# A two-layer decoder step on one core: layer norms moved behind the next projection, the input taken in quarters, a bias table written later

## The chip, the cores and the metric

The kernel runs on one core of a Trainium2 chip. A core has a matrix engine (TensorE, PE in the rows, with its weight loads as PEld), VectorE (DVE), ScalarE (ACT), GpSimd (POOL), and SyncE (SP), which here only issues transfers. All of them work on SBUF; PE writes its sums to PSUM. Sixteen DMA engines move data to and from HBM for the queues of SP, ACT and POOL. The metric is the device time of one execution in microseconds, smaller is better.

## What is computed

A decoder trunk of two layers is applied to 256 prompt rows and 64 sample rows (8 sequences of 8), 320 columns in the transposed layout that the kernel keeps (`NT = 320`); the width of the model is 2048, that is 16 tiles of 128 features. Cut to what matters:

```
layer 0: q,k,v,qi,ki,wi = h @ a_w_in; an indexer scores the keys, keeps the top k; attention; @ a_w_o
h = LN(alpha*h + mixer(h))
h = LN(alpha*h + down(silu(dwconv3(h @ w_gate)) * (h @ w_up)))        # d_ff 5504
shared k,v = h @ b_w_kv
layer 1: q = h @ b_w_q (three head groups); dilated window attention on the shared k,v; @ b_w_o
h = LN(alpha*h + mixer(h));  h = LN(alpha*h + ConvFFN(h))
LN(x) = (x - mean(x)) * rsqrt(var(x) + eps) * g + b                   # over the 2048 features
```

Everything is fp32. A T5 bias by distance (a table `rel_bias` of 32 buckets for each of 16 heads) is added to the attention logits.

## The kernel before

All projections run through one class, `Stream` (L40). A job is one projection's column block of 256 (or 512) weight columns; it is cut into chunks of 4 of the 16 feature tiles (`kc=4`), 512 KB each. `load` fetches a chunk into `raw` on the SP queue, `split` turns it into a rounded part on ACT (L82) and a remainder on DVE (L84, the tile `hl`), and `run` issues three matmuls for each 128 x 128 block: high weight by high input, high by low, low by high (L123 to L125), each over 320 columns, in fp32r, added up in a PSUM tile `acc`. A full chunk is 24 such matmuls. Up to three split and three raw chunks stand ahead of the one in work. When the last chunk of a column block is done, the job's `epi` takes `acc` out of PSUM.

Everything else is written as generators, called lanes. `run` calls `steps()` twice in each chunk, and each lane then goes on by its rate, so that attention, table building and norms stand between the chunks of the stream. A scheduler then orders each engine's instructions and may put one ahead of another; what is marked `keep_in_program_order` stays where it was written. In each engine the instructions are then executed in that order.

The order of the jobs: the indexer's keys `ki` (80 columns), its queries `qi` (4 jobs), k and v (4), q (8); then layer 0's attention over gathered pages, which uses no stream; `wo` (8 jobs); the feed-forward, in which 11 groups of up jobs (gate and up halves) alternate with 8 down jobs each; then the shared k and v (`kvb`, `vb`), 24 `qb` jobs with layer 1's attention in lanes; `wo`; the second feed-forward; and the output.

The start (L1325 to L1358): x is loaded in twelve transfers, then all 16 feature tiles are transposed by PE (48 transposes, L1353), copied by ACT to `x32` (L1354), rounded by DVE to `xh`, and the remainder goes to `xl`. Then the first job, `ki`, runs. `gen_tables` makes the bias table `tr` (16 heads by 2312 distances) and writes it to DRAM in three forms: `trd`, eight shifted copies `bsa`, and `tb` (L1380), in which each head's 384 values stand 128 times, 3 MB. Layer 0's heads read `tb` much later.

The norms: the residual `R` gets each finished column block added on DVE (L502 in `wo`, L586 in the feed-forward), and running sums `s1` (values, DVE) and `s2` (squares from ACT, added on POOL). `ln_end` (L355) reduces the sums over partitions with small matmuls (L367, L371); `ln_finish` (L376) makes mean and 1/deviation, spreads them over the partitions with more of them (L388), and `normalise` then does, tile by tile, the subtraction on DVE or POOL (L409), the scaling (L410, DVE), `xh` (L412, ACT), the shifted value (L413, ACT) and `xl` (L414, DVE). The next job multiplies `xh` and `xl`. Three norms stand before a projection in this way: after layer 0's `wo`, after its feed-forward, and after layer 1's `wo`. The fourth is followed only by the output. `ln_prepare` (L327) multiplies `R` by alpha for the next residual.

## Time and profile before

| | |
|---|---|
| time, median of 3 runs | 3316.67 us (3316.25 to 3317.85) |
| profiled execution: time, span | 3318.17 us, 3316.0 us |
| mean granted clock of TensorE | 0.981 of 2.4 GHz |
| busy: PE, PEld | 3226.7 us (97%), 3058.1 us (92%) |
| busy: DVE, ACT, POOL | 1832.6 us (55%), 1364.1 us (41%), 623.8 us (19%) |
| HBM read, written | 542.14 MB, 17.59 MB |

PE is busy for nearly all of the span, but a busy PE is not always a PE at its full rate: matmuls are pipelined (one of 320 columns lasts 0.31 us in a row and the next one starts 0.147 us later), and the granted clock is one of two levels, 1.0 (2.4 GHz) or 0.5 (1.2 GHz). So what counts is how many matmuls a stretch holds, not how busy it is.

### The profile page before, as it was taken

What the parts mean: (1) busy time and instruction counts of PE and PEld (TensorE: products, weight loads), DVE (VectorE), ACT (ScalarE), POOL (GpSimd) and SP (SyncE); (2) the same over time, 40 slices, a digit from 0 to 9 for tenths busy, and PEclk for the clock granted to TensorE, in tenths of its full rate; (3) what the DMA queues carried; (4) which work ended last, traced back from release to release, by engine and by line L of the source; (5) the groups of instructions that cost most, each with busy time, mean ns of one, the idle gap of its engine ahead of it and who ended that gap; (6) DMA issues with size and microseconds to landing.
All of it is one profiled execution on the core that took longest, in us unless ns stands there. A gap on an engine that the chain in (4) does not pass through costs nothing.

```text
span 3316.0 us, 58328 instructions
## 1 busy us (share of the span) xinstructions
PE 3226.7 (97%) x23574; PEld 3058.1 (92%) x23574; DVE 1832.6 (55%) x3170; ACT 1364.1 (41%) x2209; POOL 623.8 (19%) x820
## 2 busy tenths in 40 slices
...
GB/s 186 146 174 163 254 309 296 164 105 166 148 152 147 152 150 149 152 148 152 139 238 160 221 190 199 206 199 171 105 160 148 152 148 152 149 151 150 149 152 139
DMA packets 543249, 562.75 MB, mean 170 GB/s; under 512 B 24598, under 2 KB 520926, under 8 KB 538806
## 3 DMA queue, kind: packets, MB, share of 16 engines
...
q8 instruction: 186, 3.05, 0.4%
q14 instruction: 83, 0.68, 0.1%
HBM read 542.14 MB, written 17.59 MB: 169 GB/s over the span
## 4 chain that ended last, share of the span: by engine, by line
PE 89%; DVE 4%; DMA 3%; ACT 1%; issue 1%; POOL 0%; SPq 0%; DVEq 0%; ACTq 0%; POOLq 0%
PE acc L123 26%; PE acc L124 26%; PE acc L125 26%; PE kt L1260 1%; DMA vtb<-in_cache_v_b_dram 1%; PE s L1057 1%; PE acc L1078 1%; PE s L1213 1%; PE oa L1129 1%; DMA kx<-in_cache_kidx_a_dram,i 1%; PE s L1160 1%; DVE hl L84 1%; PE ob L1303 1%; DVE R L410 1%; DVE w L852 0%
## 5 line engine op out<-in xcount | busy, mean ns | idle before, releaser
L84 DVE TENSOR_TENSOR hl<-raw,hl 128x1024 fp32r<-128x1024 f32 (+1 forms) x752 | 927.6, 1234 | 870.8 <-ACT hl L82 867.8
L82 ACT ACTIVATE hl<-raw 128x1024 fp32r<-128x1024 f32 (+3 forms) x770 | 804.3, 1045 | 1316.9 <-PE acc L125 1123.4
L123 PE MATMUL acc<-xh,hl 128*128 128x320 f32 (+1 forms) x4176 | 1316.5, 316 | 6.6 <-ACT xh L412 5.1
L124 PE MATMUL acc<-xl,hl 128*128 128x320 f32 (+1 forms) x4176 | 1299.9, 311 | 7.2 <-DVE xl L414 7.2
L125 PE MATMUL acc<-xh,hl 128*128 128x320 f32 (+1 forms) x4176 | 1297.9, 311 | 1.5 <-POOL hl L84 1.1
L123 PEld LDWEIGHTS acc<-xh,hl 128*128 128x128 f32 (+1 forms) x4176 | 790.1, 189 | 31.0 <-issue 20.8
L124 PEld LDWEIGHTS acc<-xl,hl 128*128 128x128 f32 (+1 forms) x4176 | 789.7, 189 | 15.2 <-DVE xl L414 12.5
L125 PEld LDWEIGHTS acc<-xh,hl 128*128 128x128 f32 (+1 forms) x4176 | 789.3, 189 | 6.0 <-issue 3.5
L124 PE MATMUL acc<-H,hl 128*128 128x320 f32 x1376 | 425.4, 309 | 1.1 <-POOL H L568 1.1
L123 PE MATMUL acc<-H,hl 128*128 128x320 f32 x1376 | 426.1, 310 | 0.0
L125 PE MATMUL acc<-H,hl 128*128 128x320 f32 x1376 | 425.3, 309 | 0.3 <-DVE hl L84 0.3
L124 PEld LDWEIGHTS acc<-H,hl 128*128 128x128 f32 x1376 | 258.3, 188 | 1.6 <-POOL H L568 1.6
L125 PEld LDWEIGHTS acc<-H,hl 128*128 128x128 f32 x1376 | 258.3, 188 | 0.6 <-DVE hl L84 0.6
L123 PEld LDWEIGHTS acc<-H,hl 128*128 128x128 f32 x1376 | 258.2, 188 | 0.1
L586 DVE TENSOR_TENSOR R<-R,acc 128x320 f32<-128x320 f32 x352 | 169.9, 484 | 122.0 <-PE acc L125 121.8
L551 POOL COPY gl<-E 128x2 f32<-128x2 f32 x86 | 24.8, 288 | 1039.4 <-ACT E L547 1039.4
L568 POOL TENSOR_TENSOR H<-h,H 128x320 fp32r<-128x320 f32 x86 | 106.1, 1235 | 452.5 <-ACT H L567 438.3
L123 PE MATMUL acc<-oh,hl 128*128 128x320 f32 x512 | 161.6, 317 | 0.5 <-ACT oh L994 0.5
L124 PE MATMUL acc<-ol,hl 128*128 128x320 f32 x512 | 160.0, 313 | 0.9 <-DVE ol L995 0.9
L125 PE MATMUL acc<-oh,hl 128*128 128x320 f32 x512 | 160.0, 313 | 0.0
L1150 POOL TENSOR_TENSOR bm<-tt,pmb 128x256 f32<-128x256 f32 x48 | 45.4, 971 | 327.1 <-DVE mxb L943 310.8
L123 PEld LDWEIGHTS acc<-oh,hl 128*128 128x128 f32 x512 | 96.7, 189 | 2.8 <-ACT oh L994 1.2
(391 smaller groups left out, 3176.8 us busy)
## 6 DMA issues: line engine op xcount, KB each, us to landing
...
```

Of the source, the lines that this page charges most:

```text
L82: a = self.nc.scalar.activation(out=hl[:, 0, :m], in_=raw[:, :m], func=AF.Copy)
L84: b = eng.tensor_sub(hl[:, 1, :m], raw[:, :m], hl[:, 0, :m].bitcast(F))
L123: nc.tensor.matmul(acc[:cw, :NT], hi, xh, start=st, stop=False)
L124: nc.tensor.matmul(acc[:cw, :NT], hi, xl, start=False, stop=False)
L125: nc.tensor.matmul(acc[:cw, :NT], lo, xh, start=False, stop=sp)
L410: ve.scalar_tensor_tensor(r, r, lnp[:, d, which:which + 1], pr if d < 2 else rstd, OP.mult, OP.mult)
L568: ge.tensor_sub(lo, h, hi.bitcast(F))
L586: ve.tensor_add(r, r, acc[:, :NT])
L1057: te.matmul(p[32 * g:32 * g + 32, :], S["qsf"][:, b, 32 * g:32 * g + 32], kts[g], start=False, stop=True, tile_position=(0, 32 * g))
L1078: te.transpose(p[:, 128 * i:128 * i + 128], kr[:, o:o + 128], idf)
L1129: te.matmul(o[32 * g:32 * g + 32, 0:128], ptq[:, 128 * t + 32 * g:128 * t + 32 * g + 32], v, start=(q == 0 and t == 0), stop=(q == 4), til ...
L1150: ge.tensor_add(bm[:, g, :], tt, S["pmb"][:, g, :])
```

## The change

1. **Norms behind the projection.** The up, `kvb`, `vb` and `qb` jobs no longer take the normalised input. They take `rh` and `rl`, the two parts of the residual times the norm's gain `g`, that need no mean and no deviation (`scale_hi` on ACT, `scale_lo` on DVE), and two more columns, `g` and `b` themselves, so their matmuls have `NX = 322` columns. When a column block is done, `fix` multiplies it by 1/deviation (DVE) and adds minus mean over deviation times the product of the weights with `g` (DVE, a second instruction); the product with `b` goes in as a bias of the next step. `ln_stats` makes the statistics in a lane while the next projection runs; `ln_rest` makes the normalised residual, times alpha, later, in a lane of its own. `ln_finish` and the feed-forward's `ln_prepare` are gone. The last norm, before the output, stays as it was.
2. **x in quarters.** x is loaded in four quarters of 512 features on three queues (SP, ACT, POOL), and the first projection is now `s0`, a job of 256 indexer query columns and the 80 key columns together. After the first two quarters are transposed, its chunks alternate with the transposes of the other two. The quarters are also written to DRAM for the residual straight from ACT's queue, and the scaling of `rb` by DVE, which `tr` needs, is done there.
3. **The bias table.** `tb` is no longer written from SBUF in `gen_tables`, but by one transfer from `trd` (DRAM to DRAM), at the sixth of the eight q jobs.

Smaller ones go with these: layer 1's mixer no longer runs `ln_prepare`, the squares are added on DVE (not POOL) during `wo`, `gen_tables_b` starts after the first up jobs, and layer 1's first loads of the k and v windows are pinned.

The core of the diff:

```diff
+NX = NT + 2
...
-                    nc.tensor.matmul(acc[:cw, :NT], hi, xh, start=st, stop=False)
-                    nc.tensor.matmul(acc[:cw, :NT], hi, xl, start=False, stop=False)
-                    nc.tensor.matmul(acc[:cw, :NT], lo, xh, start=False, stop=sp)
+                    nx = job.nx
+                    nc.tensor.matmul(acc[:cw, :nx], hi, xh, start=st, stop=False)
+                    nc.tensor.matmul(acc[:cw, :nx], hi, xl, start=False, stop=False)
+                    nc.tensor.matmul(acc[:cw, :nx], lo, xh, start=False, stop=sp)
...
+    S["mr"] = sel.rearrange("p j h q -> p (j h q)").bitcast(F)[:, 0:2 * NT].rearrange("p (k n) -> p k n", k=2)
...
+    def mv_r(k):
+        lo_upto(k + 1)
+        return S["rh"][:, k, :], S["rl"][:, k, :]
+
...
-    for j in range(4):
+    job("s0", W_in, [(A_QI, 256), (A_KI, 80)], KD, mv_x, lambda i, t: epi_ki(t) if i else epi_qi(0, t))
...
             if wide:
-                job(("up", l, f0, "w"), Wu, cols[:2], KD, mv_x, lambda i, t, f0=f0: epi_up(l, f0, i, t))
+                job(("up", l, f0, "w"), Wu, cols[:2], KD, mv_r, lambda i, t, f0=f0: epi_up(l, f0, i, t), nx=NX)
             for a in range(2 if wide else 0, len(cols), 2):
                 for i in range(2):
-                    job(("up", l, f0, a + i), Wu, [cols[a + i]], KD, mv_x,
-                        lambda _, t, f=f0 + a, i=i: epi_up(l, f, i, t))
+                    job(("up", l, f0, a + i), Wu, [cols[a + i]], KD, mv_r,
+                        lambda _, t, f=f0 + a, i=i: epi_up(l, f, i, t), nx=NX)
...
+    def scale_hi(d):
+
+        se.activation(out=S["rh"][:, d, 0:NT], in_=S["R"][:, d, :], func=AF.Identity,
+                      scale=lnp[:, d, S["which"]:S["which"] + 1])
+
+    def scale_lo(d):
+        ve.scalar_tensor_tensor(S["rl"][:, d, 0:NT], S["R"][:, d, :], lnp[:, d, S["which"]:S["which"] + 1],
+                                S["rh"][:, d, 0:NT].bitcast(F), OP.mult, OP.subtract)
...
+    def lo_upto(n):
+        while S["nlo"] < n:
+            d = S["nlo"]
+            if d % 4 == 0:
+                scale_gb(d, 4)
+            scale_lo(d)
+            S["nlo"] += 1
...
+    def ln_stats(rate, mode=None):
+
+        yield
+        yield
+        tk = S["rb"]
+        ve.memset(tk, 0.0)
+        pm, pv = ps("pm"), ps("pv")
+        for p, x in ((pm, S["s1"]), (pv, S["s2"])):
+            for t, n in TG:
+                te.matmul(p[:n, t:t + 1], x[:, 128 * t:128 * t + n], ones_d[:, 0:1], start=True, stop=True)
+        m, v, rs = tk[:, 0:3], tk[:, 4:7], tk[:, 8:11]
+        for t, n in ((slice(0, 2), 128), (slice(2, 3), 64)):
+            ve.tensor_scalar(m[:n, t], pm[:n, t], -1.0, None, OP.mult)
+            ve.tensor_copy(rs[:n, t], pv[:n, t])
+        ve.tensor_mul(v, m, m)
+        ve.tensor_sub(rs, rs, v)
+        se.activation(out=rs, in_=rs, func=AF.Sqrt, bias=epst)
+        ve.reciprocal(rs, rs)
+        ve.tensor_mul(m, m, rs)
+        yield
+        yield
+        for k, x in enumerate((m, rs)):
+            p = ps("mr")
+            for t, n in TG:
+                te.matmul(p[:, 128 * t:128 * t + n], x[:n, t:t + 1].to_broadcast([n, 128]), idf[:n, :n],
+                          start=True, stop=True)
+            se.activation(out=S["mr"][:, k, :], in_=p[:, :NT], func=AF.Copy)
+        S["norm"] = lanes.add(ln_rest(mode), rate)
+        yield
+
+    def ln_rest(mode):
+
+        R, w = S["R"], S["which"]
+        for d in range(KD):
+            r = R[:, d, :]
+            ag, ab = lnq[:, d, w:w + 1], lnq[:, d, 2 + w:3 + w]
+            ve.scalar_tensor_tensor(r, r, ag, S["mr"][:, 1, :], OP.mult, OP.mult)
+            ve.scalar_tensor_tensor(r, S["mr"][:, 0, :], ag, r, OP.mult, OP.add)
+            se.activation(out=r, in_=r, func=AF.Identity, bias=ab)
+            if mode == "xs" and d % 4 == 3:
+                a = d - 3
+                se.dma_start(out=xs[1][:, a * NT:(a + 4) * NT], in_=R[:, a:a + 4, :].rearrange("p k n -> p (k n)"))
+            yield
+
+    def fix(acc, t):
+
+        if S["stats"] in lanes.lanes:
+            lanes.drain(S["stats"])
+        uv = const.tile([128, 2], F, name="uv", tag="uv", bufs=4)
+        se.activation(out=uv, in_=acc[:, NT:NX], func=AF.Copy)
+        ve.tensor_mul(t, acc[:, :NT], S["mr"][:, 1, :])
+        ve.scalar_tensor_tensor(t, S["mr"][:, 0, :], uv[:, 0:1], t, OP.mult, OP.add)
+        return uv[:, 1:2]
...
-        sq = S["fp"].tile([128, NT], F, name="sq", tag="sq", bufs=3)
+        if pool:
+            sq = S["fp"].tile([128, NT], F, name="sq", tag="sq", bufs=3)
+        else:
+            sq = ps("sq")[:, :NT]
...
-        ge.tensor_add(S["s2"], S["s2"], sq)
+        (ge if pool else ve).tensor_add(S["s2"], S["s2"], sq)
...
-        def normalise(d):
-            r = R[:, d, :]
-            if d < 2:
-                ve.tensor_sub(r, r, pm)
-            else:
-                ge.tensor_sub(r, r, m1)
-            ve.scalar_tensor_tensor(r, r, lnp[:, d, which:which + 1], pr if d < 2 else rstd, OP.mult, OP.mult)
-            bias = lnp[:, d, 2 + which:3 + which]
-            se.activation(out=S["xh"][:, d, :], in_=r, func=AF.Identity, bias=bias)
-            se.activation(out=r, in_=r, func=AF.Identity, bias=bias)
-            ve.tensor_sub(S["xl"][:, d, :], r, S["xh"][:, d, :].bitcast(F))
-            if mode == "xs" and d % 4 == 3:
-                a = d - 3
-                sy.dma_start(out=xs[1][:, a * NT:(a + 4) * NT], in_=R[:, a:a + 4, :].rearrange("p k n -> p (k n)"))
...
     def epi_wo(l, p, accs):
         for i, acc in enumerate(accs):
             d = 2 * p + i
             r = S["R"][:, d, :]
             ve.tensor_add(r, r, acc[:, :NT])
-        ln_pair(p)
+        while S["nhi"] < min(2 * p + 2, 6 * p - 18):
+            scale_hi(S["nhi"])
+            S["nhi"] += 1
+        ln_pair(p, False)
 
...
@@ -541,11 +611,14 @@
         for i, acc in enumerate(accs):
             f = f0 + i
             stc = S["stc"][:, f, :]
+            x = Fp.tile([128, NT], F, name="fx", tag="fx", bufs=4)
+            v = fix(acc, x)
+            xp, xs_ = x[:, 0:256], x[:, 256:320].rearrange("p (b t) -> p b t", t=8)
             if kind == 0:
                 e = S["E"][f % 4]
                 es = e[:, 258:338].rearrange("p (b t) -> p b t", t=10)
-                se.activation(out=e[:, 2:258], in_=acc[:, 0:256], func=AF.Copy)
-                se.activation(out=es[:, :, 2:10], in_=acc[:, 256:320].rearrange("p (b t) -> p b t", t=8), func=AF.Copy)
+                se.activation(out=e[:, 2:258], in_=xp, func=AF.Identity, bias=v)
+                se.activation(out=es[:, :, 2:10], in_=xs_, func=AF.Identity, bias=v)
                 ge.tensor_copy(es[:, :, 0:2], stc[:, 0:16].rearrange("p (b t) -> p b t", t=2))
                 gl = S["gl"][:, f // 7, :, f % 7]
                 ge.tensor_copy(gl[:, 0:2], e[:, 256:258])
...
                 h = Fp.tile([128, NT], F, name="h", tag="h", bufs=3)
-                ve.tensor_mul(h[:, 0:256], c[:, 0:256], acc[:, 0:256])
-                ve.tensor_mul(h[:, 256:320].rearrange("p (b t) -> p b t", t=8), c_sample(c),
-                              acc[:, 256:320].rearrange("p (b t) -> p b t", t=8))
+                ve.scalar_tensor_tensor(h[:, 0:256], xp, v, c[:, 0:256], OP.add, OP.mult)
+                ve.scalar_tensor_tensor(h[:, 256:320].rearrange("p (b t) -> p b t", t=8), xs_, v, c_sample(c),
+                                        OP.add, OP.mult)
...
-            ln_pair(p)
+            ln_pair(p, True, out=l)
 
...
+        S["stats"] = lanes.add(ln_stats(0.7), 1.0)
+        lanes.add(gen_lo(), 1.0)
         for key in [k for k in jobs if isinstance(k, tuple) and k[0] in ("up", "down") and k[1] == l]:
-            if key[0] == "up" and key[2] == FGROUPS[0] and prep is None:
-                prep = lanes.add(ln_prepare(), 1.0)
+            if key[0] == "down" and key[2] == key[3] == 0:
+                if S["norm"] in lanes.lanes:
+                    lanes.drain(S["norm"])
+                ln_begin_sums()
+                if l == 0:
...
-        next(g)
-        return g
+        S["stats"] = lanes.add(ln_stats(0.8, "xs"), 1.0)
+        lo_upto(4)
+        lanes.add(gen_lo(), 1.3)
+        return True
...
+    def x_load(a, b):
+        for i in (sy.dma_start(out=xn[0][:, a:b], in_=x_prompt[0, 0:128, a:b]),
+                  se.dma_start(out=xn[1][:, a:b], in_=x_prompt[0, 128:256, a:b]),
+                  ge.dma_start(out=xn[2][:64, a:b], in_=xsf[:, a:b])):
+            tc.keep_in_program_order(i)
+
+    x_load(0, 512)
+    st.load(0)
+    x_load(512, 1024)
+    st.load(1)
...
+    def x_chunk(c):
+
+        for i in range(4):
+            k = 4 * c + i
+            p = ps("xt")
+            for t in range(3):
+                n = min(128, NT - 128 * t)
+                te.transpose(p[:, 128 * t:128 * t + n], xn[t][:n, 128 * k:128 * k + 128], idf[:n, :n])
+            x = x32[c][:, i, :]
+            se.activation(out=x, in_=p[:, :NT], func=AF.Copy)
+            ve.tensor_copy(S["xh"][:, k, :], x)
+            ve.tensor_sub(S["xl"][:, k, :], x, S["xh"][:, k, :].bitcast(F))
+        se.dma_start(out=xs[0][:, 4 * c * NT:4 * (c + 1) * NT], in_=x32[c].rearrange("p k n -> p (k n)"))
+
+    warm(10)
+    x_chunk(0)
+    x_load(1024, 1536)
+    warm(4)
+    x_chunk(1)
+    tc.keep_in_program_order(ve.tensor_scalar(rb, rb, 1.0 / SCALE, None, OP.mult))
+    x_load(1536, 2048)
+    run("s0", 2)
+    x_chunk(2)
+    run("s0", 4)
+    x_chunk(3)
+    run("s0", 6)
...
-        sy.dma_start(out=tb, in_=tr[:, 1800:2184].unsqueeze(1).to_broadcast([16, 128, 384]))
-        yield
...
+        if j == 5:
+            tc.keep_in_program_order(sy.dma_start(out=tb, in_=trd[:, 1800:2184].unsqueeze(1).to_broadcast([16, 128, 384])))
```

On PE, from the last down job of layer 0 to `kvb`, the kernel before has this order (`acc` is a projection's sum, `H` the feed-forward's activations, `pm`, `pv`, `m` and `rstd` the norm's small tiles):

```order
L125 MATMUL acc<-H,hl 128x320
L367 MATMUL pm<-zero 128x4
L367 MATMUL pv<-zero 128x4
L371 MATMUL pm<-ones_d,s_8116 64x1
...
L371 MATMUL pv<-ones_d,sq 128x1 x2
L388 MATMUL m_16425<-idf,tk 128x64
...
L388 MATMUL rstd<-idf,tk 128x128 x2
L123 MATMUL acc<-xh,hl 128x320 x4
L124 MATMUL acc<-xl,hl 128x320
```

and the changed one this:

```order
L127 MATMUL acc<-H,hl 128x320
L125 MATMUL acc<-rh,hl 128x322
L126 MATMUL acc<-rl,hl 128x322
...
L388 MATMUL pm<-ones_d,s_8395 64x1
L388 MATMUL pm<-ones_d,s_8395 128x1 x2
L388 MATMUL pv<-ones_d,s_8396 64x1
...
L403 MATMUL mr<-idf,rb 128x64
L403 MATMUL mr<-idf,rb 128x128 x2
```

The norm's small matmuls, which stood between the two projections, now stand inside the second one: 36 of its matmuls come before the first group of six, and 28 more before the second; at the other two norms it is much the same.

On DVE, in that last group of down jobs, the kernel before has for one job (`s1` is the running sum, `gln` belongs to an output of the convolution):

```order
L84 TENSOR_TENSOR hl_16098<-raw_15990,hl_16098 128x1024
L216 COPY gln_16094<-gt_16117 126x128
L586 TENSOR_TENSOR R_6390<-R_6390,acc_16103 128x320
L352 TENSOR_TENSOR s1_8116<-s1_8116,R_6390 128x320
L586 TENSOR_TENSOR R_6390<-R_6390,acc_16104 128x320
L352 TENSOR_TENSOR s1_8116<-s1_8116,R_6390 128x320
```

and the changed one:

```order
L85 TENSOR_TENSOR hl_16631<-raw_16492,hl_16631 128x1024
L663 TENSOR_TENSOR R_6405<-R_6405,acc_16636 128x320
L356 SCALAR_TENSOR_TENSOR rl_16521<-R_6405,lnp_83,rh_16520 128x320
L663 TENSOR_TENSOR R_6405<-R_6405,acc_16637 128x320
L449 TENSOR_TENSOR s1_8395<-s1_8395,R_6405 128x320
L218 COPY gln_16532<-gt_16677 126x128
L449 TENSOR_TENSOR s1_8395<-s1_8395,R_6405 128x320
L356 SCALAR_TENSOR_TENSOR rl_16521<-R_6405,lnp_83,rh_16520 128x320
```

The making of `rl` has moved up into the down jobs: eight of the 16 tiles stand before the last residual is added, where no such instruction stood before.

At the start, PE has in the kernel before all 48 transposes `xt` and then `ki` (80 columns). In the changed one it has 30 of them, the last six of which belong to the third quarter, ahead of the first product:

```order
L1460 MATMUL xt<-idf,xn_110 128x64
L1460 MATMUL xt<-idf,xn_108 128x128 x3
L1460 MATMUL xt<-idf,xn_109 128x128 x3
L125 MATMUL acc<-xh,hl 128x320
L126 MATMUL acc<-xl,hl 128x320
```

So the first product moves from the 49th place behind the warming matmuls to the 31st.

## Rows read from the trace of the kernel before

**Rows 1.** Stretches (us), matmuls writing `acc` alone: length, PE busy (count), PEclk, DMA, GB/s.

```profile
0.00:60.00 60.00, 26.60 (x146) 0.77 0.70 212
692.25:740.00 47.75, 31.55 (x180) 0.75 0.25 69
1624.00:1680.00 56.00, 42.58 (x252) 0.82 0.69 205
2362.65:2420.00 57.35, 46.53 (x280) 0.85 0.31 91
```

**Rows 2.** Stretches by engine: PE, PEld, DVE, ACT, POOL busy (count), PEclk, DMA, GB/s.

```profile
715.00:1595.00 880.00, 880.00 (x5989) 879.87 (x5988) 464.10 (x625) 355.51 (x492) 80.09 (x169) 1.00 0.51 150
...
1624.00:1645.00 21.00, 16.21 (x68) 13.84 (x68) 15.00 (x22) 10.97 (x21) 13.94 (x15) 0.56 0.16 59
...
1597.00:1625.00 28.00, 27.72 (x192) 27.65 (x192) 24.37 (x41) 14.61 (x26) 16.04 (x14) 1.00 0.56 164
...
1645.00:2200.00 555.00, 548.13 (x4382) 506.81 (x4382) 274.45 (x624) 225.31 (x391) 74.84 (x106) 1.00 0.69 200
...
110.00:138.00 28.00, 26.33 (x186) 21.83 (x184) 24.32 (x70) 16.93 (x36) 8.99 (x6) 1.00 0.88 111
...
138.00:149.00 11.00, 5.40 (x25) 3.52 (x24) 5.58 (x24) 4.04 (x10) 3.40 (x4) 0.69 1.00 272
```

**Rows 3.** Timeline of PE, norm before `kvb`: start, us, instruction, count, [idle before <-releaser].

```profile
1627.59 1.31 PE L371 MATMUL pv<-ones_d,sq 128*64 128x1 f32 x6
...
1630.59 1.84 PE L388 MATMUL rstd<-idf,tk 64*128 64x64 f32 x6
...
1634.13 1.44 PE L123 MATMUL acc<-xh,hl 128*128 128x320 f32 x4 [1.70 <-ACT xh L412]
...
1638.15 0.64 PE L124 MATMUL acc<-xl,hl 128*128 128x320 f32 x1 [2.58 <-DVE xl L414]
```

**Rows 4.** Timeline of PE at the start of the kernel.

```profile
14.28 10.45 PE L1353 MATMUL xt<-idf,xn 64*128 64x64 f32 x34 [0.30 <-DMA xn<-in_x_sample_dram]
...
27.83 0.55 PE L125 MATMUL acc<-xh,hl 128*80 128x320 f32 x1 [1.13 <-POOL hl L84]
...
47.56 1.03 PE L1370 MATMUL tr<-oneh,rb 32*16 32x512 f32 x2 [3.18 <-DVE rb L1363]
...
50.16 0.47 PE L123 MATMUL acc<-xh,hl 128*128 128x320 f32 x1
...
50.42 0.47 PE L124 MATMUL acc<-xl,hl 128*128 128x320 f32 x1
```

**Rows 5.** Timelines of SP's queue, ACT and PE around the writing of `tb`.

```profile
109.79 0.68 SPq L1380 DMA_DIRECT2D tb<-tr  x1
```

```profile
142.19 0.42 ACT L764 ACTIVATE khl<-kx 128x256 fp32r<-128x256 f32 x1 [9.17 <-DMA kx<-in_cache_kidx_a_dram,i]
```

```profile
143.86 0.47 PE L771 MATMUL kt<-idr,khl 128*128 128x128 f32 x2 [5.60 <-ACT rl L782]
```

**Rows 6.** Timeline of PE, two neighbouring fp32r matmuls of 512 columns.

```profile
124.12 0.49 PE L779 MATMUL sx<-kis,qh 128*128 128x512 f32 x1
124.45 0.39 PE L780 MATMUL sx<-kis,ql 128*128 128x512 f32 x1
```

**Rows 7.** Groups of DVE instructions by line and shape: count | busy us, mean ns | idle before.

```profile
L84 DVE TENSOR_TENSOR hl<-raw,hl 128x1024 fp32r<-128x1024 f32 x720 | 899.9, 1251 | 852.9 <-ACT hl L82 849.9 <-ACT rl L782 1.1 <-DMA vtb<-in_cache_v_b_dram 0.4
...
L586 DVE TENSOR_TENSOR R<-R,acc 128x320 f32<-128x320 f32 x352 | 169.9, 484 | 122.0 <-PE acc L125 121.8
...
L410 DVE SCALAR_TENSOR_TENSOR R<-R,lnp,rstd 128x320 f32<-128x320 f32 x48 | 36.9, 806 | 2.4 <-ACT rstd L392 2.4
...
L339 DVE SCALAR_TENSOR_TENSOR R<-R,sh 128x320 f32<-128x320 f32 x64 | 29.3, 504 | 0.0
```

**Rows 8.** Timeline of PE, second matmul on the last group's third tile, layer 0.

```profile
1597.28 0.42 PE L124 MATMUL acc<-H,hl 128*128 128x320 f32 x1 [1.06 <-POOL H L568]
```

214 lines of the change are left out of this document (110 added, 104 removed).

## The prediction

> **What bounds the kernel now.** The table of busy time was read first: PE is busy for 97% of the span, no other engine for more than 55%. That alone does not say that PE runs at its rate, so the second view was a list of long stretches, and there the number of matmuls was read, not the busy time. In the first feed-forward 5989 matmuls take 880 us, 0.1469 us each, at the full clock, 2.4 GHz [rows 2]. By its jobs the kernel issues 18,192 matmuls of 320 columns in its projections; at 0.1469 us they make 2672 of the 3316 us. The reader is to see that a stretch costs too much exactly where its length is more than its count times 0.1469 us.
>
> The third view puts that to the three norms that stand before a projection [rows 1]. After layer 0's `wo`: 47.75 us with 180 projection matmuls, 47.75 - 26.4 = 21.3 us lost. Before `kvb`: 56 us with 252, 19.0 lost. After layer 1's `wo`: 57.35 us with 280, 16.2 lost. Together 56.5 us. The timeline shows what they are made of: small matmuls of the statistics, which wait for DVE and ACT in turn; waits of PE of 1.70 us for `xh` and 2.58 us for `xl`; and a clock that fell, so that the next products run slowly [rows 3], granted 0.56 over 21 us [rows 2]. A matmul of 320 columns starts 0.26 to 0.27 us after the one before at the lower level, 1.2 GHz, as at 50.16 and 50.42 [rows 4].
>
> The start is the fourth place: the products come steadily only from 27.83 us, and up to 60 us only 146 were made, worth 21.4 us [rows 1, 4]. The fifth is the `tb` write, and the wait behind it [rows 5].
>
> **The change part by part.** The sum is made against the profiled execution, 3318.17 us, which is 1.5 us above the median of the runs.
>
> *The three norms.* The next projection no longer waits for mean and deviation, and if nothing took their place the 56.5 us would go. What comes back: twelve small matmuls a norm, in place of twenty. Six took 1.31 us and six 1.84 us in rows at about half the clock [rows 3]; at the full one I take half, 1.6 us, three times: 4.7. PE would wait next for `rl`, which DVE must make before the second matmul of a block. Layer 0's last down group has DVE busy for 24.37 of 28 us [rows 2], and eight of the sixteen `rl` tiles now come before its end: 8 x 0.504 to 8 x 0.806 us, 4.0 to 6.4 us [rows 7], where 3.6 are free. So DVE ends 0.4 to 2.8 us late, and with the splits of `kvb` crowding in as much as 6; I take 2.5, and 1 at each other norm, where the sums of squares moved from POOL to DVE. Net 56.5 - 4.7 - 4.5 = 47 us saved; bounds 35 and 53. If the cover is gone (PE with nothing to multiply until the statistics end) the old loss returns.
>
> *The two columns.* 322 columns in place of 320 for the up jobs (86 tiles x 48 x 2 layers = 8256), `kvb` and `vb` (384) and `qb` (2304): 10,944 matmuls. At 0.1469/320 us a column, two columns are 0.92 ns, 10 us in all. The trace has no matmul of 322 columns. Below it could be nothing. For the upper end: two neighbouring ones of 512 columns start 0.33 us apart [rows 6], (0.33 - 0.147)/192 = 0.95 ns a column, 1.9 ns for two, 21 us. I take 10, since nearly all of these run in rows like the first of [rows 2].
>
> The page "SBUF — State Buffer" of the Trainium skill, section "Door 1: The DMA port swizzle", speaks against this part: SBUF is read in lines of 16 bytes, and each step to a new line costs something. A block of 322 values of four bytes does not start on such a line every time. No row here shows what that costs; the fourth rival weighs it.
>
> *The fix.* Each tile of up, `kvb`, `vb` and `qb` now needs two more DVE instructions: one that reads PSUM, like L586 (0.484 us), and one like L339 (0.504 us), 0.99 us [rows 7]. In a feed-forward 86 tiles: 85 us on top of 464 in 880 us [rows 2], 62% full. PE hides it, 0 us, at most 10 if the accumulators come free late. In the `qb` stretch 48 x 0.99 = 47 us come on top of 274 in 555 us [rows 2], cost 1 us, 0 to 5. Not hidden is the end of each feed-forward: PE waits 1.06 us for `H` of the last group [rows 8], and the fix stands in just that chain. Two tiles, 2 x 0.99 us, twice: 4 us, 0 to 8.
>
> *x in quarters.* Before, the 34 last transposes run from 14.28 us at 10.45/34 = 0.31 us each [rows 4], so 14 were done by then. With 30 ahead of the first product, and the first two quarters landing no later, the same pace gives 14.28 + 16 x 0.31 = 19.2 us; with three queues and no wait for the second quarter about 17.5. From 27.83 that is 8.6 to 10.3 earlier. The 18 other transposes now stand between the products and still cost PE 18 x 0.15 to 18 x 0.31, 2.8 to 5.5 us. The wait for `rb`, 3.18 us [rows 4], goes with the scaling moved ahead, and with it the slow matmuls after it, from 49.6 to 53 us, some 14 x 0.12 = 1.7 us. Against it stand the splits and roundings that DVE must now do between the chunks, 2 us by choice. 9.5 - 4.2 + 3.2 + 1.7 - 2 = 8 us saved, bounds 4 (products at 19.2, DVE twice as late) and 16 (DVE never late, transposes at the full clock, and the 20 products that ran at the lower clock from 27.83 on, 2.4 us, faster too). The transfer of the third quarter stands on ACT's queue behind ACT's copies; if it lands late, PE waits and the clock falls.
>
> *The table.* `tb` is asked for at 109.79 us; the DMA engines are 88% busy up to 138 us, and ACT waits 9.17 us for the gathered `kx`, PE 5.60 us in turn [rows 5, 2]. Then the clock is granted at 0.69 over 11 us [rows 2]; I put 2 us on it. 7.5 saved, 3 to 9. In its new place the write stands on SP's queue among the loads of the q jobs. It takes some 32 us (109.79 to 142), in which the stream wants 512 KB per 24 matmuls, that is per 3.5 us. Up to six chunks are ahead, 21 us; if nothing else got through, 32 - 21 = 11 us would be lost. The burst moved 111 GB/s [rows 2], where another stretch reaches 272, so both share: I take 1, bounds 0 and 11. What is queued behind it on SP is the next `raw` loads, and PE waits for those.
>
> **Sum.** 3318.2 - 47 + 10 + 4 + 1 - 8 - 7.5 + 1 = 3271.7; less the 1.5 us to the median, 3270 us.
>
> **Rivals.**
>
> *A, slower: columns charged in steps.* 0.1469 us is 352.6 ticks of 2.4 GHz for 320 columns, so something beyond a tick a column is paid. If it is paid for each block of 32 columns, an eleventh block for two columns costs 13.3 ns, x 10,944 = 146 us, and the time is 3270 - 10 + 146 = 3406. The place is every up, `kvb`, `vb` and `qb` matmul. All other terms together save 56.5 us, so it decides from 56.5/10,944 = 5.2 ns a matmul. For: the excess over a tick a column. Against: at 1.2 GHz 320 columns take 0.267 us [rows 4], one tick a column with no steps.
>
> *B: DVE becomes the bound behind each norm.* In the 70 us after a norm DVE has 20 splits (25 us), eight `rl`, ten fixes (10 us), and `ln_rest` with 32 instructions of 0.504 to 0.806 us (16 to 26): with the work it has already, 60 to 74 us. For: L410, of the same form, takes 0.806 us beside POOL's work, not 0.504 [rows 7]. Against: `ln_rest` is spread over a lane of its own. PE then loses up to 7 us a norm, 3270 + 21 = 3291.
>
> The skill's same page, section "Who interferes with whom", says that a DVE instruction with two SBUF inputs contends with a GpSimd instruction that reads SBUF. By that rule, the 0.806 us of L410 agree: POOL is busy for 13.94 of the 21 us of that stretch [rows 2].
>
> *C: start and table give nothing.* The third quarter lands late, or DVE paces the first chunks, and the `tb` burst loses in the q jobs what it lost before: 3270 + 8 + 7.5 = 3285. For: the DMA engines are already 70% busy over the first 60 us [rows 1], and DVE must do roundings and splits in turn. Against: the stream's chunks stand far ahead in the q jobs.
>
> *D: the wider tiles are read more slowly.* Each block of 322 columns begins at an uneven place, and PE pays for that more than the two columns: at the slope of the pair of 512 columns, 1.9 ns, it is 21 us in place of 10, 3281. For: that pair [rows 6]. Against: the steady 0.1469 us [rows 2]. The skill's rule on lines of 16 bytes is of this kind: 1288 bytes touch 81 lines at the least, 1280 touched 80; by that rule alone two columns would cost 1/80 of 0.1469 us, an estimate of 1.8 ns, 20 us in all.
>
> **How the numbers follow.** The forecast has 0.50, A 0.06, B 0.17, C 0.14, D 0.13. The range that holds 8 in 10 is 3252 to 3298: below, the start at its upper bound (8 more) and columns that cost nothing (10); above, B's 3291 with the upper ends of the fix and `qb` terms (8 more, rounded). C and D lie inside. What is left out is A and the two tails. 0.2% is 6.6 us, what a measurement of this kernel can tell from no change: faster needs less than 3310. The forecast, B, C and D all lie under it; B and C together, with a burst that costs its 11, come to 3270 + 21 + 15.5 + 10 = 3316, for which 0.03 is taken from theirs. A lies above. Faster 0.91, within 0.2% 0.03, slower 0.06.
>
> **What would show it.** In the up jobs matmuls start 0.1478 us apart; 0.1469 or 0.149 would move the sum by 10 us. Around the three norms, the stretches' lengths come to count times that price plus some 3 us, with the clock granted at 1.00. The first product starts at 17 to 20 us, and no wait for `rb` follows. No idle time of 5.6 us near 140 us, and none for `raw` in the sixth to eighth q jobs. The wait for `H` of the last group grows from 1.06 to about 3 us. Wrong would be: a spacing over 0.152 us (A), PE waiting for `rl` or `acc` behind DVE for more than 5 us at a norm (B), the products of `s0` broken by waits for `xt` or `xh` (C).

## The result: slower, where a gain was forecast

The changed kernel takes 3337.5 us (median of five runs, 3332.2 to 3345.4), the kernel before 3316.7 beside it: a ratio of 1.0074, interval 1.0060 to 1.0088. Repeated later, beside other runs of the kernel before, it came to 1.0071 (1.0054 to 1.0088). The forecast was 3270, in 3252 to 3298.

The page of the changed kernel: span, busy time by engine, clock in 40 slices.

```profile
span 3337.1 us, 58894 instructions
PE 3225.2 (97%) x23526; PEld 3060.8 (92%) x23526; DVE 2068.1 (62%) x3703; ACT 1409.4 (42%) x2433; POOL 611.0 (18%) x754
PEclk9999999999999999999999999999999999999999
```

PE is busy as long as before, and its clock is higher (0.988, was 0.981). Nothing here says where 21 us went. The stretches that answer to [rows 1] are more telling (columns as there).

```profile
0.00:60.00 60.00, 33.50 (x200) 1.00 0.65 196
714.00:760.00 46.00, 35.19 (x219) 0.93 0.35 94
1646.00:1700.00 54.00, 42.87 (x248) 0.91 0.67 205
2390.00:2447.00 57.00, 52.97 (x350) 1.00 0.46 133
```

The start holds 200 projection matmuls where 146 were, and the third norm's stretch 350 where 280 were; 57 us can hold some 385 at 0.148 us each. The second norm's, 248 in 54 us, is as poor as before. The first product comes at 22.28 us; ahead of it PE waits for the third quarter of x:

```profile
21.73 0.90 PE L1460 MATMUL xt<-idf,xn 128*128 128x128 f32 x3 [3.17 <-DMA xn<-in_x_prompt_dram]
```

**A ledger.** Both kernels issue 18,192 projection matmuls, in the same order but for the first 144 and some hundred places where two within a chunk are swapped. So the start of the n-th one in one trace can be set against the n-th in the other, and the growth of the difference over a stretch is what that stretch lost (+) or gained (-), in us. It is worked out from the start times in the timelines of PE, one profiled execution each. `changed_again` is the changed kernel once more, and `rest_slower` (below) has its instructions in the same order on PE, DVE, ACT and GpSimd, from the first to the last; these two, the repeats, show how far the rows move by themselves.

| matmuls, stretch | changed | changed_again | rest_slower | tb_unpinned | gather_index_early | table_b_held | copies_pinned | four_mended | second_norm_pinned | second_norm_stride_324 |
|---|---|---|---|---|---|---|---|---|---|---|
| to 192, start | -10.8 | -10.9 | -11.1 | -10.6 | -12.0 | -12.0 | -11.8 | -8.9 | -11.3 | -10.3 |
| to 336, indexer | +13.2 | +13.7 | +12.8 | +12.7 | +5.8 | +12.6 | +12.9 | +5.8 | +5.8 | +5.6 |
| to 768, indexer, k, v | -9.3 | -9.3 | -9.3 | -4.4 | -9.3 | -9.3 | -9.3 | -4.6 | -4.3 | -4.1 |
| to 1535, q | +25.4 | +22.5 | +25.2 | -0.6 | +22.5 | +25.2 | +24.5 | -0.2 | -0.3 | +1.9 |
| to 2304, attention, `wo` | -1.5 | +0.8 | -12.5 | -4.6 | -13.3 | -2.4 | -1.5 | +4.4 | +0.6 | +3.3 |
| to 2784, first norm | -4.9 | -5.9 | -5.6 | -6.1 | -5.9 | -15.4 | -2.5 | -10.7 | -15.2 | -15.8 |
| to 8496, feed-forward | +9.0 | +9.0 | +9.0 | +9.0 | +9.0 | +9.0 | +9.0 | +9.0 | +9.0 | +5.2 |
| to 9024, second norm | -0.1 | -1.8 | -1.4 | -1.8 | 0.0 | -2.3 | -6.7 | -8.2 | -6.5 | -9.3 |
| to 11904, `qb`, `wo` | +5.9 | +8.5 | +6.6 | +7.2 | +5.6 | +7.3 | +10.9 | +6.6 | +7.0 | +4.9 |
| to 12240, third norm | -11.8 | -11.8 | -11.8 | -11.8 | -11.8 | -11.8 | -7.1 | -7.1 | -11.5 | -11.9 |
| to 18191, feed-forward | +6.4 | +6.6 | +6.7 | +6.5 | +6.7 | +6.9 | +5.6 | +5.6 | +6.5 | +6.5 |
| sum | +21.5 | +21.5 | +8.8 | -4.5 | -2.8 | +8.0 | +23.8 | -8.3 | -20.4 | -24.0 |

In the three columns of the changed kernel's order the rows lie within 3 us of each other, but for the attention row, which moves by 13 us with no edit in it. It seems to go with the chip: `rest_slower`, `stats_later`, `gather_index_early` and `tb_unpinned` ran on one where the kernel before also took less, 3307.5 us, and no trace of the kernel before was taken there. So a time is best compared with a run of the changed kernel's order on the same chip. Four rows of the first column are off the forecast by far: the q jobs, the indexer, and the first and second norm.

**The q jobs.** The waits of PE from 60 to 400 us (what was waited for: us in total, times, longest), and PE's timeline:

```profile
PE pc L937 <- DVE w L933: 20.6, 15, 4.0
PE s L1139 <- DVE ms L973: 5.8, 1, 5.8
PE kit L787 <- ACT qh L801: 4.9, 1, 4.9
```

```profile
320.32 0.16 PE L937 MATMUL pc<-cnt,pair 128*128 128x1 f16 x1 [1.05 <-DVE w L933]
324.44 0.16 PE L937 MATMUL pc<-cnt,pair 128*128 128x1 f16 x1 [3.96 <-DVE w L933]
326.63 0.16 PE L937 MATMUL pc<-cnt,pair 128*128 128x1 f16 x1 [2.02 <-DVE w L933]
...
336.32 0.16 PE L937 MATMUL pc<-cnt,carry 128*128 128x1 f16 x1 [1.51 <-DVE w L933]
...
343.81 0.58 PE L1139 MATMUL s<-ms,sel 128*128 128x256 bf16 x2 [5.83 <-DVE ms L973]
344.04 0.61 PE L125 MATMUL acc<-xh,hl 128*128 128x320 f32 x1
```

`pc` is the counting step of the sample top-k, a chain in which PE and DVE wait for each other, in 34 steps. In the kernel before, 18 or 24 projection matmuls stand between two steps and hide it. In the changed one the last seven steps stand together, and the last 120 matmuls of the q jobs behind them. They come at 344 us, after 25 us in which PE does almost nothing, and begin at the lower clock (0.55 is granted from 344 to 349 us).

### The profile page after: what moved, and what is told of

It reads as the page before. It is cut to its first block, busy times and chain, and to the rows that moved or that the text cites. A ratio compares the mean times of both kernels' runs of the same rounds, so it can differ in the third digit from the quotient of the medians.

```text
span 3337.1 us, 58894 instructions
## 1 busy us (share of the span) xinstructions
PE 3225.2 (97%) x23526; PEld 3060.8 (92%) x23526; DVE 2068.1 (62%) x3703; ACT 1409.4 (42%) x2433; POOL 611.0 (18%) x754
## 4 chain that ended last, share of the span: by engine, by line
PE 45%; DVE 3%; DMA 2%; issue 1%; ACT 0%; SPq 0%; POOL 0%; DVEq 0%; ACTq 0%; POOLq 0%
PE acc L125 14%; PE acc L127 13%; PE acc L126 13%; PE kt L1351 1%; PE s L1304 1%; DMA vtb<-in_cache_v_b_dram 1%; PE ob L1394 1%; DVE hl L85 1%; PE s L1246 1%; DMA krb<-in_cache_k_b_dram 1%; DVE s L449 0%; PE s L1245 0%; DVE R L415 0%; PE pt L1382 0%; SPq L1281 0%
## 5 line engine op out<-in xcount | busy, mean ns | idle before, releaser
L85 DVE TENSOR_TENSOR hl<-raw,hl 128x1024 fp32r<-128x1024 f32 (+2 forms) x756 | 923.1, 1222 | 738.6 <-ACT hl L83 737.0
L83 ACT ACTIVATE hl<-raw 128x1024 fp32r<-128x1024 f32 (+2 forms) x772 | 803.5, 1041 | 1114.7 <-PE acc L127 935.8
L125 PE MATMUL acc<-rh,hl 128*128 128x322 f32 x3648 | 1153.2, 316 | 5.4 <-ACT hl L83 3.2
L127 PE MATMUL acc<-rh,hl 128*128 128x322 f32 x3648 | 1135.4, 311 | 5.2 <-DVE hl L85 5.2
L126 PE MATMUL acc<-ol,hl 128*128 128x322 f32 (+1 forms) x3264 | 1016.8, 312 | 0.9 <-DVE ol L1081 0.9
L125 PEld LDWEIGHTS acc<-rh,hl 128*128 128x128 f32 x3648 | 689.9, 189 | 18.0 <-issue 13.8
L127 PEld LDWEIGHTS acc<-rh,hl 128*128 128x128 f32 x3648 | 690.9, 189 | 9.7 <-DVE hl L85 6.5
L126 PEld LDWEIGHTS acc<-ol,hl 128*128 128x128 f32 x3264 | 618.7, 190 | 2.2 <-DVE ol L1081 1.2
L126 PE MATMUL acc<-rl,hl 128*128 128x322 f32 x896 | 281.0, 314 | 0.0
L126 PEld LDWEIGHTS acc<-rl,hl 128*128 128x128 f32 x896 | 171.5, 191 | 1.9 <-issue 1.2
L125 PE MATMUL acc<-xh,hl 128*128 128x320 f32 (+1 forms) x528 | 171.8, 325 | 0.7 <-ACT kit L739 0.7
L126 PE MATMUL acc<-xl,hl 128*128 128x320 f32 (+1 forms) x528 | 166.4, 315 | 0.0
L127 PE MATMUL acc<-xh,hl 128*128 128x320 f32 (+1 forms) x528 | 165.0, 313 | 0.0
```

The lines of the kernel that those rows point to most:

```text
L83: a = self.nc.scalar.activation(out=hl[:, 0, :m], in_=raw[:, :m], func=AF.Copy)
L85: b = eng.tensor_sub(hl[:, 1, :m], raw[:, :m], hl[:, 0, :m].bitcast(F))
L125: nc.tensor.matmul(acc[:cw, :nx], hi, xh, start=st, stop=False)
L126: nc.tensor.matmul(acc[:cw, :nx], hi, xl, start=False, stop=False)
L127: nc.tensor.matmul(acc[:cw, :nx], lo, xh, start=False, stop=sp)
```

## The experiments

Edits are against the changed kernel. Ratios are to the kernel before, run beside each.

**The held write.**

```diff
         if j == 5:
-            tc.keep_in_program_order(sy.dma_start(out=tb, in_=trd[:, 1800:2184]...))
+            sy.dma_start(out=tb, in_=trd[:, 1800:2184]...)
```

> The changed kernel with one word less: the write of tb from DRAM is no longer held at its written place among the q jobs. In the trace of the changed kernel 120 products of the last q job (1416 to 1536) stand behind the seven last counting steps of the sample top-k, so PE waits for VectorE 20.6 us there; unpinned they stand between those steps again, as in the kernel before. Theory (the pin sets an order in which PE works through a serial chain without cover): the products 1344 to 1416 lose nothing, 25 us come back, about 3312 us, and the products 200 to 340 and all norms are as in the changed kernel. Rival (the burst of the write itself starves the stream, wherever it stands): it moves the loss to the k and v jobs, gain under 5 us, about 3334 us.

3314.8 us, ratio 1.0025 (1.0016 to 1.0034). The 25 us are gone from the q jobs (+25.4 to -0.6), and PE works through the same window, as the changed kernel's row and this one's show:

```profile
318.00:344.00 26.00, 4.10 (x22) 0.56 0.05 18
```

```profile
318.00:344.00 26.00, 25.25 (x174) 1.00 0.43 127
```

Not all of it is won. The write, when not held, goes out at 130.00 us, among the k and v jobs, and costs 4.9 us there (-9.3 to -4.4):

```profile
130.00 0.63 SPq L1617 DMA_DIRECT2D tb<-trd  x1
```

And 8 us come back in the attention row (-4.6, where `rest_slower` on the same chip has -12.5): two of the 34 steps and six other small products now stand there. The whole gain is 11 us by the medians against `rest_slower` (3326.1 to 3314.8), 13 by the ledger. So the theory's mechanism holds and its 25 us do not; the rival's gain under 5 us is not seen either. In the changed kernel DMA is busy for 0.05 of that stretch: no transfer starved PE.

**The late gather.** In the changed kernel GpSimd's gathers of the index keys start at 58.69 us, before at 38.62:

```profile
58.69 2.17 POOL L823 DMA_INDIRECT kx<-in_cache_kidx_a_dram,i  x1 [46.95 <-DVE kin L759]
```

They need row numbers from DVE, which the program computes behind the first projection; `s0` has 144 matmuls where `ki` had 48. The edit (the generator and its tile move up with it):

```diff
     x_load(1536, 2048)
+    for _ in gen_rows("i8", 2):
+        pass
     run("s0", 2)
...
     run("s0")
-    for _ in gen_rows("i8", 2):
-        pass
```

> The changed kernel with the row numbers of the key gather computed by VectorE ahead of the first products, not behind the first projection. Theory (in the changed kernel these stand behind s0, three times as long as ki was, so the gathers are issued at 58.7 us, 20 us later than before, ACT waits 5.0 + 1.8 us for them ahead of the copies of qh, PE idles 4.9 us and its clock falls to 0.70): the gap at 67 to 73 us goes with the slow stretch behind it, 10 to 13 us, about 3326 us. Rival (ACT's queue is behind anyway, or the gathers only wait for the memory that the x tiles free): the gathers start no earlier than 50 us and the gain is under 3 us, 3335 us.

3319.1 us, ratio 1.0037 (1.0023 to 1.0050). The gathers start at 44.48 us:

```profile
44.48 1.05 POOL L823 DMA_INDIRECT kx<-in_cache_kidx_a_dram,i  x1 [33.03 <-DVE kin L758]
```

7.4 us come back (+13.2 to +5.8), not 10 to 13. Most of the other 5.8 is work that moved: ten `tr` products and three of `kit`, which before stand among the first 192 matmuls, stand in this stretch now. Against `rest_slower`, on the same chip, the time is 7.0 us less (3326.1 to 3319.1).

**Statistics later, residual slower.** `stats_later`, and below it `rest_slower`:

```diff
     def ln_stats(rate, mode=None):
+        yield
+        yield
```

```diff
-        S["stats"] = lanes.add(ln_stats(0.7), 1.0)
+        S["stats"] = lanes.add(ln_stats(0.35), 1.0)
-        S["stats"] = lanes.add(ln_stats(0.8, "xs"), 1.0)
+        S["stats"] = lanes.add(ln_stats(0.4, "xs"), 1.0)
```

> The changed kernel with the sums' small matmuls two steps (some 24 products) later in the next projection, at all three norms. Theory (PE waits for the running sums that a late VectorE has not finished: 1.7 + 1.2 + 3.4 us at the first norm, 2.0 at the second, and the clock falls behind both): these waits go, 6 to 9 us at the first norm and 2 to 4 at the second, nothing at the third; about 3327 us. Rival (VectorE is the bound there, and the wait only moves to the splits of the weights): under 2 us gained, 3336 us.

> The changed kernel with the lane that makes the normalised residual going at half its rate at all three norms. Theory (its three instructions a tile crowd the splits of the weights out on VectorE and ScalarE: PE waits 3.2 and 1.9 us for the split weights at the second norm and 1.9 + 0.5 at the first, then runs at the lower clock): these waits go, 5 to 9 us in all, about 3330 us; the waits for the sums stay. Rival (the work is only put off, to where the lane is drained ahead of the first down job): the same us are lost there, 3337 us.

The first: 3323.4 us, ratio 1.0049 (1.0035 to 1.0063); the first norm -8.3 in place of -4.9, the second +1.3 in place of -0.1. That is two us together where 8 to 13 were expected, and none against `rest_slower`. The wait moved to the splits, as the rival said: PE's wait for DVE's part of a split grew from 2.4 to 4.3 us behind the first norm and from 1.9 to 4.8 behind the second. The second: 3326.1, ratio 1.0058 (1.0044 to 1.0072). With the rate halved the scheduler put every engine's instructions in the same order as before the edit, so this says nothing on the theory and is a repeat of the changed kernel. What both times gained is the attention row (-11.7 and -12.5).

**The width.** The core of `narrow_320`, and below it that of `stride_324`:

```diff
-                    nx = job.nx
+                    nx = NT
```

```diff
+NS = 324
...
-        return S["rh"][:, k, :], S["rl"][:, k, :]
+        return S["rh"][:, k, 0:NX], S["rl"][:, k, 0:NX]
...
-        S["rh"], S["rl"], S["nlo"] = cols3(big("rh", FR), NX), S["ol"], 0
+        S["rh"], S["rl"], S["nlo"] = cols3(big("rh", FR), NS), S["ol"], 0
```

> The changed kernel with 320 columns in every matmul, the rows of rh and rl still 322 wide; what is left out are the two columns for the norm's g and b, so the corrections use other values. In the changed kernel a matmul of 322 columns starts on average 149.2 ns after the one before, one of 320 in the same run 147.6, and from matmul 2784 to 8160 (the first feed-forward) 7.9 us are lost on the kernel before. Theory (the two columns themselves cost it): the spacing falls to 147.6 ns and the stretch loses 1 us or less. Rival (rows that start at uneven places): the spacing stays at 149 ns and the stretch loses 7 us still.

> The changed kernel with 322 columns as it has them, but rows of 324 in SBUF, so that each starts at a multiple of 16 bytes (a buffer of the indexer has three copies in place of four to make room). Theory (the columns cost it, not where a row starts): the spacing stays at 149.2 ns, the first feed-forward loses 7.9 us still. Rival (uneven starts): the spacing falls to 148.5 ns (147.6 and two columns at 0.46 ns), the stretch loses 3.8 us plus 1.

One execution each: 3322.8 and 3341.0 us. The count of matmuls in 700 us of either feed-forward, for the kernel before, the changed kernel, `narrow_320`, `stride_324`:

```profile
850.00:1550.00 700.00, 700.00 (x4775) 1.00 0.51 150
2500.00:3200.00 700.00, 700.00 (x4774) 1.00 0.51 150
```

```profile
850.00:1550.00 700.00, 700.00 (x4726) 1.00 0.50 149
2500.00:3200.00 700.00, 700.00 (x4749) 1.00 0.50 149
```

```profile
850.00:1550.00 700.00, 700.00 (x4776) 1.00 0.50 150
2500.00:3200.00 700.00, 700.00 (x4741) 1.00 0.50 149
```

```profile
850.00:1550.00 700.00, 700.00 (x4748) 1.00 0.50 149
2500.00:3200.00 700.00, 700.00 (x4748) 1.00 0.50 149
```

Before it is 146.6 ns a matmul in either (700/4775). Of a feed-forward's matmuls two thirds are up jobs (4128 of 6192), so 700/4726 = 148.1 ns means 2.3 ns more for each of 322 columns in the first, and 700/4749 = 147.4 means 1.2 in the second. With rows of 324 it is 1.2 in both. Taken one by one from the start times behind the ledger, the up jobs' matmuls start 146.7 ns apart before (either feed-forward), 148.9 and 148.1 in the changed kernel, 146.6 and 148.3 in `narrow_320`, 147.9 and 148.2 in `stride_324`; the 149.2 and 147.6 of the expectations are not the spacing in a feed-forward. So two columns cost 1.2 to 1.5 ns, against 0.92 by the share of columns, and uneven rows can double it. They need not: 320 columns on rows of 322 cost nothing in the first feed-forward and 1.6 ns in the second. In us, where the changed kernel has +9.0 and +6.4, `narrow_320` has +0.5 and +7.1, `stride_324` +5.2 and +6.5: both theories fit one feed-forward only. Why one and not the other is not settled; the tiles lie at other places in it.

**How much VectorE has to do.** `less_sums`, and below it `squares_on_pool`:

```diff
-        ve.tensor_add(S["s1"], S["s1"], R[:, d, :])
```

```diff
-        ln_pair(p, False)
+        ln_pair(p, True)
```

> The changed kernel with the running sum of the values left out (VectorE adds nothing to s1; the mean is wrong): 15 instructions of about 0.48 us less on VectorE ahead of each norm, nothing else moved. In the changed kernel the products behind the first norm (2352 to 2784) lose 8.3 us, those behind the second (8544 to 9024) 9.0 us. Theory (VectorE as a whole is the bound there, busy for 10.00 of 10 us in the slices ahead of both): 7 us less work take the waits for the sums, the clock's fall and the late splits with them: 2 to 3 us lost behind each. Rival (the order of the instructions and ScalarE's and PE's queues make the waits, not the amount): 6 us or more are lost still.

> The changed kernel with the squares added on GpSimd during wo, as in the kernel before, not on VectorE: 15 instructions less on VectorE ahead of the first and third norm. Theory (VectorE is the bound behind the first norm, and this move of the change filled it): the 8.3 us lost from 2352 to 2784 fall to 3 to 4, and the second norm and the third stay as they are. Rival (GpSimd's adds are slower and slow VectorE's two-input instructions beside them by as much): 7 us or more lost still.

One execution each. `less_sums`, 3330.6 us: second norm -6.2 in place of -0.1 (-1.4 and -1.8 in the repeats), as the theory said; first norm -5.5 in place of -4.9 (-5.6 and -5.9), nothing. So at the first norm it is not the amount of work. At the second it may be; but there, against what was expected, the edit also moved instructions of PE, ScalarE and DVE to other places, so amount and order are not told apart. `squares_on_pool`, 3344.4 us: first norm -2.9, worse by 2 to 3. The third norm shows what else: there DVE makes `rl` and the sums in the same way, and PE waits 0.9 us in all. GpSimd is idle there. At the first it is building the second bias table. DVE's timeline across it, then GpSimd's, in the changed kernel:

```profile
698.85 2.79 DVE L356 SCALAR_TENSOR_TENSOR ol<-R,lnp,rh 128x320 fp32r<-128x320 f32 x1
...
704.33 1.93 DVE L356 SCALAR_TENSOR_TENSOR ol<-R,lnp,rh 128x320 fp32r<-128x320 f32 x4
...
708.62 3.20 DVE L356 SCALAR_TENSOR_TENSOR ol<-R,lnp,rh 128x320 fp32r<-128x320 f32 x1
...
717.64 3.86 DVE L85 TENSOR_TENSOR hl<-raw,hl 128x1024 fp32r<-128x1024 f32 x1
```

```profile
697.42 3.87 POOL L682 TENSOR_TENSOR sb<-trb,mk 16x1024 f32<-16x1024 f32 x1
...
708.32 3.14 POOL L682 TENSOR_TENSOR sb<-trb,mk 16x1024 f32<-16x1024 f32 x1
...
717.34 3.07 POOL L682 TENSOR_TENSOR sb<-trb,mk 16x1024 f32<-16x1024 f32 x1
```

Between GpSimd's adds four tiles of `rl` (written over `ol` here) take 1.93 us, 0.54 each with a little overlap. A tile that DVE begins while L682 runs ends only after it: L682 ends at 701.29 and 711.46, the tiles at 701.64 and 711.82, 0.35 us later both times. The split begun at 717.64 takes 3.86 us, not 1.21, and ends 1.09 us after L682. So DVE is not slower there, it stands still until GpSimd's add is over; the 1.1 to 1.4 us of the expectation below are means of four tiles, of which one stood still. The edit holds that table at its written place:

```diff
-            ge.dma_start(out=mk, in_=c_smaskb[q:q + 1]...)
+            tc.keep_in_program_order(ge.dma_start(out=mk, in_=c_smaskb[q:q + 1]...))
-            ge.tensor_add(sb[:, 0:512], ...)
+            tc.keep_in_program_order(ge.tensor_add(sb[:, 0:512], ...))
```

> The changed kernel with GpSimd's building of the second bias table held at its written place (two instructions of each of its eight rounds are pinned), so that only two rounds stand ahead of the first up jobs, not seven. In the changed kernel these rounds run from 686 to 735 us, across the first norm, and VectorE's making of rl takes 1.1 to 1.4 us a tile there instead of 0.54, one split 3.86 us instead of 1.21; at the third norm GpSimd is idle and nothing is lost. Theory (GpSimd's adds beside VectorE's instructions of two SBUF inputs make VectorE late behind the first norm): the 8.3 us lost from product 2352 to 2784 fall to 2 to 4, rl takes 0.5 to 0.6 us a tile, the second norm stays. Rival (the waits come from how much VectorE has to do and in which order, as GpSimd's work was there before too): 7 us or more are lost still.

One execution, 3325.3 us: first norm -15.4 in place of -4.9. PE, DVE and ScalarE have their instructions in the order of the changed kernel, from the first to the last; GpSimd's alone moved. That leaves the rival, amount and order of DVE's work, no room here. All engines from 700 to 720 us, changed and with the table held:

```profile
700.00:720.00 20.00, 15.77 (x106) 15.19 (x104) 20.00 (x23) 7.03 (x9) 15.03 (x13) 1.00 0.48 126
```

```profile
700.00:720.00 20.00, 20.00 (x137) 19.31 (x136) 13.88 (x30) 9.06 (x13) 0.00 (x0) 1.00 0.49 138
```

DVE finishes 30 instructions in 13.88 us instead of 23 in 20. This is the rule that the prediction named, of the Trainium skill's page "SBUF — State Buffer", "Who interferes with whom": a DVE instruction with two SBUF inputs contends with a GpSimd instruction that reads SBUF. The trace agrees: the instruction ended 0.35 us (a tile) and 1.09 us (a split) after GpSimd's add.

**ScalarE's order at the second norm.** The changed kernel:

```profile
1658.51 0.30 ACT L395 ACTIVATE rb<-rb,epst 128x3 f32<-128x3 f32 x1 [3.06 <-DVE rb L394]
1662.05 0.44 ACT L405 ACTIVATE sel<-mr 128x320 f32<-128x320 f32 x1 [3.25 <-PE mr L403]
...
1665.04 0.56 ACT L417 ACTIVATE R<-R,lnq 128x320 f32<-128x320 f32 x1 [1.54 <-DVE R L416]
...
1666.30 1.04 ACT L83 ACTIVATE hl<-raw 128x1024 fp32r<-128x1024 f32 x1
```

ACT waits for PE's `mr` with the next split, L83, queued behind it; PE then waits for that split, 3.2 us, and 1.9 more for DVE's part. The edit:

```diff
-            se.activation(out=S["mr"][:, k, :], in_=p[:, :NT], func=AF.Copy)
+            tc.keep_in_program_order(se.activation(out=S["mr"][:, k, :], in_=p[:, :NT], func=AF.Copy))
...
-            ve.scalar_tensor_tensor(r, r, ag, S["mr"][:, 1, :], OP.mult, OP.mult)
+            tc.keep_in_program_order(ve.scalar_tensor_tensor(r, r, ag, S["mr"][:, 1, :], OP.mult, OP.mult))
-            se.activation(out=r, in_=r, func=AF.Identity, bias=ab)
+            tc.keep_in_program_order(se.activation(out=r, in_=r, func=AF.Identity, bias=ab))
```

> The changed kernel with ScalarE's copies of mr and the first and third instruction of each tile of the normalised residual held at their written place. In the order of ScalarE two weight splits then stand ahead of the copies behind the second norm, where none stood; at the first and third norm the order stays. Theory (behind the second norm ScalarE waits for the statistics' chain with the next chunk's split queued behind it, and PE in turn waits 3.2 + 1.9 us for that split, after which its clock falls): these waits go, and the 9.0 us lost from product 8544 to 9024 fall to 3 to 5. Rival (the split would come late anyway, because VectorE or the weights' transfer is late): 8 us or more are lost still.

One execution, 3341.9 us. Two splits now stand ahead of the copies (`copies_pinned`, ACT):

```profile
1658.95 2.05 ACT L83 ACTIVATE hl<-raw 128x1024 fp32r<-128x1024 f32 x2
1663.77 0.44 ACT L405 ACTIVATE sel<-mr 128x320 f32<-128x320 f32 x1 [2.77 <-PE mr L403]
```

PE's waits for that split are gone. The second norm gains 6.6 us (-0.1 to -6.7; 5 against the repeats), the first loses 2.4, the third 4.7 and `qb` 2 to 5. Held everywhere, it is not worth it.

**Together.** The four diffs that `tb_unpinned`, `gather_index_early`, `table_b_held` and `copies_pinned` show, and the changed kernel beside them:

> The changed kernel with four edits together: the tb write not held, the gather's row numbers early, the second bias table held, the copies pinned. Theory (the losses add up from stretches that do not overlap: 20 + 7.5 + 5 + 5 us): 37 us under the changed kernel, ratio to the kernel before 0.996, some 3303 us where that one takes 3316. Rival (one wait mended hands its time to the next): less than 25 us under the changed kernel, not faster than the kernel before, ratio 1.000 or more.

> The changed kernel as it is, beside the same runs of the kernel before, so that the kernel with four edits has a partner. Both theories: ratio 1.006 to 1.009.

3307.3 us, ratio 0.9976 (0.9965 to 0.9987): faster than the kernel before by 8 us, and below the changed kernel by 0.0095, some 31 us of the 37 expected. Then the holding only where it helped, and nothing held in the residual's lane (the edit is against the kernel with four edits); and the same with rows of 324:

```diff
-            tc.keep_in_program_order(se.activation(out=S["mr"][:, k, :], in_=p[:, :NT], func=AF.Copy))
+            i = se.activation(out=S["mr"][:, k, :], in_=p[:, :NT], func=AF.Copy)
+            if mode == "xs":
+                tc.keep_in_program_order(i)
```

> The kernel with four edits, with only the copies of mr behind the second norm held, and nothing held at the first and third norm and in the residual's lane. Where copies of mr and residual were held at all three, 7.5 us were gained behind the second norm, and some 4 us lost behind the first (product 2496 to 2784), 4.5 behind the third (12096 to 12240). Theory (these losses are the price of the holding there, by the same mechanism the other way): both go, the gain at the second norm stays within 2 us; 8 us under the kernel with four edits, ratio 0.994 to 0.996. Rival (they come from the later start of the residual's lane at any norm, or the second norm's gain came from holding the residual): ratio 0.997 or more.

> The same with rows of 324 for the 322 columns. In the first feed-forward these cost 4.3 us where rows of 322 cost 7.9, in the second 5.6 and 5.4. Theory (rows at even places help only where the tile's place makes the uneven ones cost more): 3 to 4 us gained in the first feed-forward, none in the second, ratio 0.001 below that of the run beside it. Rival (the difference belonged to the other changes of place that the wider rows bring): no gain.

3300.9 us, ratio 0.9957 (0.9943 to 0.9970), and 3294.3 us, ratio 0.9942 (0.9928 to 0.9956). Both theories hold: the losses at the first and third norm go, the gain at the second stays (-6.5); the wider rows give 3.8 us in the first feed-forward and none in the second. The intervals of the last two overlap; the ledger tells them apart. Both beat the kernel before and the changed one.

## Why the prediction was wrong

Three of its steps failed, and a fourth term was too small. The sum forecast 46.5 us less than before (3271.7 against 3318.2), the ledger has 21.5 more. Of the 68 us between, 30 lie at the norms, 24 in the q jobs, 9 ahead of them, 4 in the feed-forwards and 2 over `qb` and `wo`; the attention row gives 1.5 back.

1. *"In its new place ... I take 1, bounds 0 and 11."* It weighed the write as traffic, 32 us of it. From DRAM its packets took 12.7 us (303.29 to 316.01), and PE waited for none of it in the q jobs. What cost 25 there was the order: holding one transfer let the scheduler put 120 matmuls behind a serial chain that they had hidden. With what the attention row and the k and v jobs take back, 11 to 13 us of the whole time hang on the holding. The order stood in PE's list before anything ran (1410 matmuls ahead of a step, then 1416 ahead of each of seven); the prediction read the order at the norms and at the start only.
2. *"8 us saved"* at the start, and 7.5 from the old write. With the gather mended the first 768 matmuls gain 15.5 us, as much as these two: 6.2 in the first 336, 9.3 behind. The way there was another, so the match is in part luck. The first product came at 22.28 us, not at 17 to 20, because PE waited for the third quarter, as rival C has it (the row is shown with the result). Behind it PE waited for no `xh`, `xl` or split up to 62 us, where 2 us were charged. The step left out that what was written behind `ki` now stands behind three times as many matmuls: DVE's row numbers, and with them the gathers, 20 us later, cost 7.4.
3. *"Net ... 47 us saved"* at the norms. 16.8 were (-4.9, -0.1, -11.8); what failed is the 4.5 put on DVE's lateness. Rival B named DVE late behind the norm, beside GpSimd, and priced it at 7 us a norm by the amount of DVE's work. At the first norm it was some 10 (table held), and by DVE standing still for GpSimd, not by the amount. At the second 5 to 6.6 go with ScalarE's order, and 4 to 6 with `less_sums`, which changed amount and order. At the third, with neither, 11.8 of 16.2 came. "1 at each other norm" had no row of GpSimd behind it. Mended, the three give 33 to 37, so the 47 was too high also; what keeps the rest was not tested.
4. *The two columns*, 10 us: 13 in the two feed-forwards alone, where 7.6 were forecast. Rival D's mechanism was seen for 322 columns in the first only. Rival A fell: 2.3 ns a matmul at most, where 5.2 decide.
5. Right were the third norm's mechanism, the fix at no cost within the first feed-forward (`narrow_320` has it too, and loses 0.5), and three waits gone or absent: for the old `tb`, for `rb`, and for `raw` in the last q jobs. The tail of a feed-forward grew by 1 us each, not 2, and the wait for `H` from 1.1 to 1.4 us in the first, not to 3.

Not covered by any experiment: 5.9 us over `qb` and `wo` (6.6 and 8.5 in the repeats).
